# Two token streams in one transformer kernel: the context stream's mixer and feed-forward part moved beside the latent feed-forward part, and every engine's order set by a list scheduler

## The chip, the cores and the metric

The kernel runs on one core of one Trainium2 chip. The metric is the device time of one execution in microseconds (us). Three runs of the kernel before gave 1917.36, 1915.74 and 1923.25 us, a median of 1917.36.

## The reference, cut to what matters

Two layers work on two streams of tokens: 512 latent tokens (x) and 256 context tokens (ctx), both 1024 wide, with the same weights. All of it is float32.

```python
for i in range(DEPTH):                                   # DEPTH = 2
    h_l = rmsnorm(x, norm1_g[i]) * (1.0 + sc1_l) + sh1_l
    h_c = rmsnorm(ctx, norm1_g[i]) * (1.0 + sc1_c) + sh1_c
    p_l = h_l @ w_in[i]
    p_c = h_c @ w_in[i]
    ...
    k_all = jnp.concatenate([k_c, k_l], axis=1)          # latent queries read context and latent keys
    v_all = jnp.concatenate([v_c, v_l], axis=1)
    att_l = diff_attention(q_l, k_all, v_all, lam, subln_g[i], lam_init)
    x = x + g1_l * mix_out(p_l, att_l, hy_params, sg_params, w_out[i])   # hyena | sgu | attention
    x = x + g2_l * swiglu(rmsnorm(x, norm2_g[i]) * (1.0 + sc2_l) + sh2_l, ffn_w1[i], ffn_w2[i])
    if not last:
        att_c = diff_attention(q_c, k_c, v_c, lam, subln_g[i], lam_init)
        ctx = ctx + g1_c * mix_out(p_c, att_c, hy_params, sg_params, w_out[i])
        ctx = ctx + g2_c * swiglu(rmsnorm(ctx, norm2_g[i]) * (1.0 + sc2_c) + sh2_c, ffn_w1[i], ffn_w2[i])
return x
```

A mixer has three head groups: a long convolution done by small Fourier matrices (hyena), a gated spatial mixing (sgu) and differential attention. In layer 0 both streams go through everything. In layer 1 the context stream gives only its keys and values. So nothing of the latent stream in layer 0 needs more of the context stream than its keys and values of layer 0, and the rest of the context stream's layer 0 is first needed for its keys and values of layer 1.

## The kernel before

**Arithmetic.** Activations stand transposed, 128 of the width on the partitions and the tokens along the row. Each float32 operand is split in a high and a low part (`split`, L232 on ACT and L233 on DVE, some on POOL), and a product is three matmuls (`mm3`, L251 to L253) of one 128x128 block each, 512 columns wide for the latent stream and 256 for the context stream and for token-major projections. Weights arrive by DMA from the SP queue into `FW` (L240) and are split into `RW`, which holds three pairs of 128x1024.

**Tasks.** The program is written as Python generators that give up control at small steps: `lat_task` (latent stream), `con_task` (context stream), `side_task` (the filters' spectra, L905 and L906) and `ada_task` (modulation vectors, matmuls of L400). `woven` always resumes the one that has the smallest cost counted so far, divided by a rate; the rates are the tables `CON`, `SIDE`, `ADA` by phase, and `WOVEN` inside the latent mixer. So the tables and the code's order decide in which order work is written down; the tile framework's scheduler then sets each engine's order from it and places the waits. Every engine runs its queue in order.

**Stages.** From 0 to about 612 us the mixers of both streams in layer 0 run woven together: the latent one by `lat_mixer`, the context one by `con_front` (keys, queries, values, attention), `hyena`, `sgu` and `outproj`. From about 612 to 1195 us one `ffn` serves both streams in layer 0: a weight block is loaded and split once, then used for 512 latent and 256 context columns (six rounds of hidden blocks, `ROUNDS[1]`). From 1195 to 1550 us the latent mixer of layer 1 runs, with the context's keys and values in it, and from 1550 us to the end the latent FFN of layer 1 (four rounds).

**Places that the prediction names.** `norm` sums squares with a matmul against ones (L279), takes a reciprocal root in small DVE steps (`rsqrt`, L261 to L267) and spreads it with transposes (L293). In `attend`, scores take three matmuls over 64 partitions, then DVE takes the maximum (L686), ACT the exponential (L691), DVE joins the two halves (L697), and PE transposes the result (L706). `fwd` of the hyena ends in adds on DVE (L1037) and splits (L1039, L1041) on which the next matmuls wait. `AHEAD` says for how many hidden blocks the first half of the tokens is done before the second half's norm is ready ("W": weights in `RW`, "R": weights kept in `R`): one in layer 0, four in layer 1. `POOL` says which element-wise work goes to GpSimd.

## Time and profile before

| | us |
|---|---|
| median of three runs | 1917.36 |
| the profiled execution's own time | 1918.05 |
| its span, first to last instruction | 1916.3 |
| TensorE (PE) busy in it | 1797.2 |
| VectorE (DVE) busy | 1079.3 |
| ScalarE (ACT) busy | 676.9 |
| GpSimd (POOL) busy | 118.0 |

The mean granted TensorE clock was 0.963 of full speed. HBM was read at 221.18 MB and written at 22.41 MB over the span. Matmuls are pipelined and their ends are modelled in the records: one matmul lasts longer than the step to the next one's start, so the busy time of PE says where it stood still, not how fast it could be.

### The profile page before, as it was taken

To read this page: it belongs to the slowest core of one execution; us is meant where nothing else is said; L and a number is where in the kernel's file an instruction comes from. 1 tells how busy PE (TensorE), PEld (TensorE's weight loads), DVE (VectorE), ACT (ScalarE), POOL (GpSimd) and SP (SyncE) were. 2 spreads that over 40 slices of the span, in tenths; PEclk is the share of its full clock that TensorE was granted. 3 is DMA by queue.
4 is the path that set the end of the run, shared out by engine and by line. 5 is a ranking of instruction groups with operands and counts; after the bars stand their busy time and mean duration, and the time that the engine had idled before them with its cause. 6 is when DMAs were issued, how large, how long until landed. Compare 5 with 4: busy or idle time off the path is not lost.

```text
span 1916.3 us, 27513 instructions
## 1 busy us (share of the span) xinstructions
PE 1797.2 (94%) x10938; PEld 1532.3 (80%) x10938; DVE 1079.3 (56%) x2243; ACT 676.9 (35%) x1167; POOL 118.0 (6%) x127
## 2 busy tenths in 40 slices
PE   4799898888997999999999999899999999999999
PEld 1478798677776888888888888789988798888887
DVE  5677786876868533332323244779588773333333
ACT  2534434443535321212121222633455452222221
POOL 1100223311001000000000000011000000000000
PEclk9799899799997999999999999899999899999999
DMA  8667644335454434343424135453213222323321
GB/s 274 198 222 237 212 155 133 111 101 162 144 174 137 153 99 136 90 136 110 149 86 146 61 112 174 138 171 124 72 43 111 73 62 64 115 83 102 93 93 65
DMA packets 101819, 245.39 MB, mean 128 GB/s; under 512 B 9748, under 2 KB 21750, under 8 KB 101690
## 3 DMA queue, kind: packets, MB, share of 16 engines
q1 hardware_dynamic: 93450, 221.71, 36.3%
q0 software_dynamic: 8240, 21.92, 3.9%
q8 instruction: 86, 1.41, 0.3%
q14 instruction: 43, 0.35, 0.1%
HBM read 221.18 MB, written 22.41 MB: 127 GB/s over the span
## 4 chain that ended last, share of the span: by engine, by line
PE 72%; DVE 7%; ACT 2%; issue 1%; DMA 1%; POOL 0%; DVEq 0%; ACTq 0%
PE banks L251 23%; PE banks L252 22%; PE banks L253 22%; PE banks L706 1%; PE banks L400 1%; DVE tiny L686 1%; PE banks L279 1%; DMA F<-x_ctx 1%; DVE F L459 1%; DVE RW L233 0%; ACT F L506 0%; ACT F L691 0%; DVE F L1028 0%; DVE F L1189 0%; DVE F L1026 0%
## 5 line engine op out<-in xcount | busy, mean ns | idle before, releaser
L251 PE MATMUL banks<-R,RW 128*128 128x512 f32 (+1 forms) x1984 | 698.3, 353 | 8.1 <-ACT R L507 2.9
L252 PE MATMUL banks<-R,RW 128*128 128x512 f32 (+1 forms) x1984 | 695.2, 351 | 2.6 <-DVE R L510 2.6
L253 PE MATMUL banks<-R,RW 128*128 128x512 f32 (+1 forms) x1984 | 693.4, 350 | 1.7 <-DVE RW L233 1.7
L232 ACT ACTIVATE RW<-FW 128x1024 fp32r<-128x1024 f32 (+2 forms) x240 | 240.3, 1002 | 563.9 <-PE banks L252 427.5
L251 PEld LDWEIGHTS banks<-R,RW 128*128 128x128 f32 x1984 | 379.0, 191 | 66.8 <-issue 5.6
L252 PEld LDWEIGHTS banks<-R,RW 128*128 128x128 f32 x1984 | 378.8, 191 | 51.9 <-DVE R L510 3.9
L253 PEld LDWEIGHTS banks<-R,RW 128*128 128x128 f32 x1984 | 378.1, 191 | 50.1 <-DVE RW L233 2.1
L233 DVE TENSOR_TENSOR RW<-FW,RW 128x1024 fp32r<-128x1024 f32 (+2 forms) x228 | 263.1, 1154 | 243.5 <-ACT RW L232 225.7
L1189 DVE SCALAR_TENSOR_TENSOR F<-banks,mods,F 128x512 f32<-128x512 f32 (+1 forms) x192 | 116.3, 615 | 177.1 <-PE banks L253 150.6
L251 PE MATMUL banks<-R 128*128 128x256 f32 (+3 forms) x584 | 185.0, 336 | 30.7 <-ACT R L1039 12.3
L252 PE MATMUL banks<-RW,R 128*128 128x256 f32 x624 | 178.9, 287 | 2.3 <-DVE RW L233 2.2
L251 PE MATMUL banks<-RW,R 128*128 128x256 f32 x624 | 180.1, 289 | 0.8 <-ACT RW L232 0.7
L253 PE MATMUL banks<-RW,R 128*128 128x256 f32 x624 | 179.0, 287 | 0.0
L252 PE MATMUL banks<-R 128*128 128x256 f32 (+3 forms) x584 | 176.6, 316 | 0.0
L253 PE MATMUL banks<-R 128*128 128x256 f32 (+3 forms) x584 | 175.2, 312 | 1.3 <-DVE R L1041 1.3
L251 PEld LDWEIGHTS banks<-R 128*128 128x128 f32 (+1 forms) x584 | 114.8, 205 | 55.9 <-ACT R L1039 14.6
L1207 DVE TENSOR_TENSOR F<-F,banks 128x256 f32<-128x256 f32 (+1 forms) x71 | 40.0, 565 | 203.8 <-PE banks L253 189.9
L232 ACT ACTIVATE R<-F 128x512 fp32r<-128x512 f32 (+1 forms) x133 | 71.8, 550 | 222.9 <-DVE F L1207 159.8
L252 PEld LDWEIGHTS banks<-R 128*128 128x128 f32 (+1 forms) x584 | 117.5, 205 | 8.8 <-issue 3.0
L252 PEld LDWEIGHTS banks<-RW,R 128*128 128x128 f32 x624 | 120.8, 194 | 4.6 <-DVE RW L233 3.7
L251 PEld LDWEIGHTS banks<-RW,R 128*128 128x128 f32 x624 | 120.8, 194 | 3.7 <-issue 1.0
L253 PEld LDWEIGHTS banks<-RW,R 128*128 128x128 f32 x624 | 120.9, 194 | 0.7 <-issue 0.2
(158 smaller groups left out, 1681.1 us busy)
## 6 DMA issues: line engine op xcount, KB each, us to landing
FW<-in_ffn_w SPq DMA_DIRECT2D x104, 512.0 KB, 3.7
FW<-in_ada_w SPq DMA_DIRECT2D x96, 512.0 KB, 5.3
FW<-in_w_in_tm SPq DMA_DIRECT2D x50, 512.0 KB, 4.7
R<-in_tab POOLq DMA_DIRECT2D x28, 512.0 KB, 5.9
FW<-in_w_in_cm SPq DMA_DIRECT2D x24, 512.0 KB, 4.7
F<-x_ctx SPq DMA_DIRECT2D x36, 256.0 KB, 3.4
FW<-in_ffn_w SPq DMA_DIRECT2D x24, 384.0 KB, 3.1
x_ctx<-F SPq DMA_DIRECT2D x32, 256.0 KB, 2.4
```

Source lines behind the costliest of these rows:

```text
L232: self.nc.scalar.activation(hi, src, AF.Copy)
L233: (lo_eng or self.nc.vector).tensor_tensor(lo, src, hi.bitcast(F32), op=ALU.subtract)
L251: mm(out, lhsT=lh, rhs=rh, start=(i == 0), stop=False)
L252: mm(out, lhsT=lh, rhs=rl, start=False, stop=False)
L253: mm(out, lhsT=ll, rhs=rh, start=False, stop=(i == n - 1))
L279: nc.tensor.matmul(p1[:, t:t + 1], lhsT=sq[:, t * P:(t + 1) * P], rhs=self.ones[:, 0:1], start=True, stop=True)
L400: nc.tensor.matmul(pa[32 * j:32 * j + 32, :], lhsT=self.cv[:, k, :], rhs=ws[j // 2][:, j % 2, z], start=(k == 0), stop=(k == KT - 1), tile ...
L459: nc.vector.tensor_tensor(st.acc[:, cols], st.acc[:, cols], q.ap, op=ALU.add)
L686: nc.vector.tensor_reduce(m, b.ap, axis=AX.X, op=ALU.max)
L706: nc.tensor.transpose(p[:, i, z, :], ws[z][:, (a + i) * P:(a + i + 1) * P], self.ident)
L1189: self.nc.vector.scalar_tensor_tensor(x, p, self.mods[l][:, sec * 8 + k, st.v:st.v + 1], x, op0=ALU.mult, op1=ALU.add)
L1207: nc.vector.tensor_tensor(s.ap, s.ap, u, op=ALU.mult)
```

## The change

**What is computed when.** `con_front` gives only keys and values in layer 0, as in layer 1, and writes them to DRAM. The context stream then waits for "lat mixed", which the latent stream sets after the first halves of its FFN blocks. Only then it loads ctx again, norms it a second time, loads its keys and values, and does queries (`queries`, new), attention, sgu, hyena, output projection, second norm and its own FFN, and then the norm, keys and values of layer 1. All this is written between the latent stream's FFN of layer 0 and the start of its mixer of layer 1. The two streams' FFNs of layer 0 are two calls now, in four rounds each: every weight block of that layer is loaded and split twice. The latent FFN of layer 0 has four hidden blocks ahead, as layer 1 had. The spectra for 256 and for layer 1 also wait for "lat mixed". All work of POOL but one of the hyena's products (8 multiplies) goes to DVE.

**Who sets the order.** The program's calls are no longer issued as they come: `Plan` notes them all, works out from the memory they touch which needs which, gives each a duration, and plays the five engines forward; on each engine it always takes, of the calls that are ready, the one with the lowest rank (three quarters its place in the code, one quarter the length of what hangs on it). Then it issues them in that order and ties each call to the one before on its engine, so that the framework keeps the order. All instructions now have the line of `issue` (L1611).

```diff
-ROUNDS = [[(0, 6), (6, 6), (12, 5), (17, 5)], [(0, 4), (4, 4), (8, 4), (12, 4), (16, 3), (19, 3)]]
+ROUNDS = [[(0, 6), (6, 6), (12, 5), (17, 5)]]
...
-CON = [9.69, 5.75, 2, 0.75, 1.53, 5, 22.61]
+CON = [4, 5.75, 2, 6, 40, 20, 22.61]
...
+BESIDE = 14.0
+PAUSE = 12.0
...
-        "parity": (1, 0),
-        "product 1": (1, 1),
-        "product 2": (1, 0),
-        "mix": (0, 2)}
+POOL = {"in cm": (0, 0), "in tm": (0, 0), "out": (0, 0), "rope": (0, 0), "parity": (0, 0),
+        "product 1": (1, 0), "product 2": (0, 0), "mix": (0, 0)}
...
-AHEAD = ["W", "RRRW"]
+AHEAD = ["RRRW", "RRRW"]
...
+    def queries(self, st, l, j, rope):
+
+        n = st.T // 64
+        yield from self.claim(n)
+        st.held[j] += n
+        yield from self.room(*[2] * st.nt, 2)
+        gq = self.qk(st, l, 5 + j, 0, rope)
+        st.q[j] = next(gq)
...
+class Plan:
...
+    PE, DVE, ACT, POOL, SP = range(5)
+    RATE, LINE, HANDOVER, DRAIN, LANDING, WINDOW = 2.4, 258.0, 38.0, 163.0, 1620.0, 3413.0
+    COLD, WARM, ROWS = 0.5, 0.9, 100.0
...
+        rank = [self.share * k / n - (1 - self.share) * rest[k] / top for k in range(n)]
...
+    def issue(self):
+
+        nosync = mybir.DependencyInfo(mybir.DependencyClass.NoSync, mybir.DependencyReason.DATA)
+        last = [None] * 5
+        for k in self.order():
+            e, calls = self.todo[k][:2]
+            for op, args, kw in calls:
+                ins = getattr(getattr(self.tc.nc, Program.engines[e]), op)(*args, **kw).ins
+                if last[e] is not None:
+                    self.tc.add_manual_dep(ins, last[e], nosync, reason="order")
+                last[e] = ins.name
...
-        yield from con_front(0, False)
-        yield from net.hyena(con, 0, kd[0, CTX], ready=lambda: wait((0, CTX)))
-        yield from net.sgu(con, 0)
+        yield from con_front(0)
+        yield from wait("lat mixed")
+        yield from net.room(2, 2, 2, 2)
+        net.load_x(con)
+        yield from start(con, 0, 0, True)
+        for j in range(2):
+            yield from net.kv_load(con, j, kvd[0])
+            yield from net.queries(con, 0, j, False)
+            yield from net.attend(con, 0, j, [con])
...
+        yield from net.sgu(con, 0)
+        yield from net.hyena(con, 0, kd[0, CTX], ready=lambda: wait((0, CTX)))
         net.drop_h(con)
...
-        yield from mark("con")
-        yield from wait("ffn")
+        net.rates["con"] = BESIDE
+        yield from net.pause(PAUSE)
+        yield from net.ffn([con], 0, ROUNDS[0], (), True)
...
-        ff = net.ffn([lat, con], 0, ROUNDS[1], AHEAD[0], True, lambda: wait("con"))
+        ff = net.ffn([lat], 0, ROUNDS[0], AHEAD[0], True)
         yield from lat_mixer(0, ff, WOVEN[0])
         phase(3)
+        yield from take(ff, len(AHEAD[0]))
+        done.add("lat mixed")
```

**Three places in the order of PE.** In the names, `R` and `RW` hold split activations and weights, `F` unsplit ones, `ones` and `inv` belong to a norm, `ident` is the identity for transposes, and `banks` is where sums are gathered. The number at the end of a row is how many equal instructions follow each other.

The first norm of layer 1, where the latent FFN of layer 0 ends. Before:

```order
L252 MATMUL banks<-R,RW 128x256
L253 MATMUL banks<-R,RW 128x256
L279 MATMUL banks<-ones_102,F 128x1 x6
L293 MATMUL banks<-ident_100,inv 128x128 x4
L251 MATMUL banks<-R,RW 128x512 x3
L252 MATMUL banks<-R,RW 128x512
```

After:

```order
L1611 MATMUL banks<-R,RW 128x512
L1611 MATMUL banks<-R,RW 128x256 x62
L1611 MATMUL banks<-ones_86,F 128x1
L1611 MATMUL banks<-R,RW 128x256
L1611 MATMUL banks<-ones_86,F 128x1 x3
L1611 MATMUL banks<-R,RW 128x256 x17
L1611 MATMUL banks<-ident_85,inv 128x128 x4
L1611 MATMUL banks<-R,RW 128x256 x13
L1611 MATMUL banks<-R,RW 128x512 x14
L1611 MATMUL banks<-R,RW 128x256 x15
```

Between the ones-matmuls and the `inv` transposes of the latent norm stood nothing; now the context FFN's matmuls (256 columns) stand there, 17 in a row, 62 ahead of it and 13 behind it.

The end of the latent mixer of layer 0: the last steps of the latent attention, from the last scores to the first matmuls of what follows. Before:

```order
L252 MATMUL banks<-R 128x256
L253 MATMUL banks<-R 128x256
L706 MATMUL banks<-ident_100,F 128x128 x8
L905 MATMUL banks<-R 128x512
L706 MATMUL banks<-ident_100,F 128x128 x4
L906 MATMUL banks<-R 128x512
L905 MATMUL banks<-R 128x512
L251 MATMUL banks<-R 128x256
```

After:

```order
L1611 MATMUL banks<-R 128x256 x14
L1611 MATMUL banks<-ident_85,F 128x128
L1611 MATMUL banks<-R 128x256
L1611 MATMUL banks<-ident_85,F 128x128 x6
L1611 MATMUL banks<-R 128x256 x12
L1611 MATMUL banks<-ident_85,F 128x128 x4
L1611 MATMUL banks<-R 128x256 x18
L1611 MATMUL banks<-ones_86,F 128x1 x2
L1611 MATMUL banks<-R 128x256 x3
L1611 MATMUL banks<-ones_86,F 128x1 x2
L1611 MATMUL banks<-R 128x256 x34
L1611 MATMUL banks<-ident_85,inv 128x128 x4
```

Before, the `ident` transposes of the last attention (L706) had only single matmuls of the spectra (L905, L906) beside them. Now latent FFN matmuls of 256 columns, with weights kept in `R`, stand around them: the rows of 14, 1, 12, 3, 34 are the FFN's, the row of 18 is the attention's own product.

The latent FFN of layer 0. Before, with both streams on the same weights:

```order
L251 MATMUL banks<-R,RW 128x512
L252 MATMUL banks<-R,RW 128x512
L253 MATMUL banks<-R,RW 128x512
L251 MATMUL banks<-R,RW 128x256
L252 MATMUL banks<-R,RW 128x256
L253 MATMUL banks<-R,RW 128x256
```

After, in the part where the context's attention runs:

```order
L1611 MATMUL banks<-R,RW 128x512 x3
L1611 MATMUL banks<-R 128x256 x5
L1611 MATMUL banks<-R,RW 128x512 x12
L1611 MATMUL banks<-ident_85,F 128x128
L1611 MATMUL banks<-R,RW 128x512 x5
L1611 MATMUL banks<-ident_85,F 128x128 x3
L1611 MATMUL banks<-R,RW 128x512 x4
L1611 MATMUL banks<-R 128x256
L1611 MATMUL banks<-R,RW 128x512 x6
L1611 MATMUL banks<-R 128x256 x5
L1611 MATMUL banks<-ones_86,F 128x1 x2
L1611 MATMUL banks<-R,RW 128x512 x2
```

Before, PE had 512 and 256 columns of the same weights in turn; now the latent FFN's matmuls of 512 columns surround the scores, transposes (`ident`) and products of the context's attention.

## Rows read from the trace of the kernel before

**Rows 1.** Page, part 1: busy us (share of the span) xinstructions
```profile
PE 1797.2 (94%) x10938; PEld 1532.3 (80%) x10938; DVE 1079.3 (56%) x2243; ACT 676.9 (35%) x1167; POOL 118.0 (6%) x127
```

**Rows 2.** Windows by stretch: us, each engine's busy us (xinstructions), PEclk, DMA share, GB/s
```profile
0.00:96.00 96.00, 57.78 (x280) 30.74 (x281) 60.03 (x134) 40.62 (x73) 12.24 (x21) 0.86 0.71 236
96.00:612.00 516.00, 462.46 (x3200) 392.22 (x3199) 381.86 (x923) 225.53 (x428) 78.85 (x76) 0.93 0.52 165
612.00:1195.00 583.00, 581.71 (x3556) 506.01 (x3555) 215.07 (x338) 134.30 (x209) 8.54 (x11) 1.00 0.38 120
1195.00:1550.00 355.00, 333.51 (x2137) 296.58 (x2136) 279.14 (x640) 174.68 (x309) 18.33 (x19) 0.94 0.33 103
1550.00:1908.00 358.00, 357.97 (x1757) 303.88 (x1756) 141.74 (x210) 101.80 (x148) 0.00 (x0) 1.00 0.28 86
1908.00:1916.30 8.30, 3.80 (x17) 2.81 (x15) 1.50 (x2) 0.00 (x0) 0.00 (x0) 1.00 0.15 63
```

**Rows 3.** Timeline, PE, FFN of layer 1: start us, us, engine, line, form
```profile
1639.64 0.39 PE L251 MATMUL banks<-R,RW 128*128 128x512 f32 x1
...
1644.85 0.39 PE L253 MATMUL banks<-R,RW 128*128 128x512 f32 x1
```

**Rows 4.** Timeline, PE, FFN of layer 0
```profile
699.76 0.28 PE L251 MATMUL banks<-R,RW 128*128 128x256 f32 x1
...
703.96 0.28 PE L253 MATMUL banks<-R,RW 128*128 128x256 f32 x1
704.17 1.07 PE L400 MATMUL banks<-FW,cv 128*32 128x256 f32 x16
```

**Rows 5.** Groups by line and form, PE: xcount | busy us, mean ns | idle before
```profile
L251 PE MATMUL banks<-R,RW 128*128 128x512 f32 x1200 | 473.5, 395 | 3.8 <-ACT R L507 2.9 <-ACT F L555 0.9
L251 PE MATMUL banks<-R,RW 128*128 128x256 f32 x784 | 224.7, 288 | 4.2 <-DVE F L1189 2.4 <-DVE R L233 1.0 <-ACT R L232 0.8
L251 PE MATMUL banks<-RW,R 128*128 128x256 f32 x624 | 180.1, 289 | 0.8 <-ACT RW L232 0.7
L251 PE MATMUL banks<-R 128*128 128x256 f32 x432 | 129.6, 310 | 19.8 <-ACT R L1039 8.6 <-ACT R L507 3.9 <-ACT F L691 3.8
L400 PE MATMUL banks<-FW,cv 128*32 128x256 f32 x768 | 71.5, 421 | 23.7 <-DMA FW<-in_ada_w 23.7
```

**Rows 6.** Waits of PE, 96 to 612: us in total, times, longest
```profile
PE banks L251 <- ACT R L1039: 7.4, 4, 3.7
PE banks L706 <- DVE F L697: 5.9, 4, 4.0
PE banks L706 <- DVE F L482: 4.0, 1, 4.0
```

**Rows 7.** Windows around two norms and the last attention
```profile
576.00:612.00 36.00, 25.13 (x120) 19.93 (x121) 27.47 (x73) 18.12 (x39) 5.05 (x7) 0.72 0.50 154
1200.00:1224.00 24.00, 16.14 (x71) 13.31 (x70) 18.68 (x52) 13.18 (x21) 0.53 (x1) 0.72 0.51 142
1512.00:1548.00 36.00, 29.05 (x154) 25.70 (x151) 27.75 (x69) 22.19 (x47) 0.00 (x0) 0.72 0.13 41
```

**Rows 8.** Waits of PE, 0 to 96
```profile
PE banks L400 <- DMA FW<-in_ada_w: 17.7, 6, 9.5
PE banks L859 <- DMA F<-in_feats: 8.0, 1, 8.0
```

**Rows 9.** Groups by line and form, DVE and ACT: splits and multiplies
```profile
L233 DVE TENSOR_TENSOR RW<-FW,RW 128x1024 fp32r<-128x1024 f32 x172 | 211.8, 1232 | 200.5 <-ACT RW L232 182.9 <-PE banks L400 11.5 <-DMA FW<-in_ada_w 4.2
L232 ACT ACTIVATE RW<-FW 128x1024 fp32r<-128x1024 f32 x184 | 194.6, 1059 | 451.2 <-PE banks L252 334.1 <-PE banks L253 43.3 <-issue 42.7
L233 DVE TENSOR_TENSOR RW<-FW,RW 128x768 fp32r<-128x768 f32 x40 | 38.2, 954 | 26.1 <-ACT RW L232 26.0
L232 ACT ACTIVATE RW<-FW 128x768 fp32r<-128x768 f32 x40 | 33.8, 845 | 75.1 <-PE banks L252 62.5 <-issue 7.8 <-DMA FW<-in_w_out 3.9
```

**Rows 10.** DMA issues of the whole run: xcount, KB each, us to landing
```profile
FW<-in_ffn_w SPq DMA_DIRECT2D x104, 512.0 KB, 3.7
```

More of the change, by code (lines that the diff above doesn't have):

```diff
@@ L1 @@
+import heapq
 import math
@@ L127 @@
 UNITS = {"R": 104, "RW": 24, "F": 44, "FW": 24}
-CON = [9.69, 5.75, 2, 0.75, 1.53, 5, 22.61]
-SIDE = [2.59, 3, 8.68, 2.5, 5.1, 16.97, 0.64]
-ADA = [3.0, 0.6, 1.74, 0.52, 8.5, 2, 2]
+CON = [4, 5.75, 2, 6, 40, 20, 22.61]
+SIDE = [2.59, 3, 2, 4, 5.1, 16.97, 0.64]
+ADA = [3.0, 0.6, 1.74, 0.9, 8.5, 2, 2]
+BESIDE = 14.0
+PAUSE = 12.0
 WOVEN = [[11.5, 12.75, 10.55, 5.68, 7.8, 6.8, 3.47, 5.43, 8.37, 16.82],
          [8.7, 11.57, 10, 5.22, 3.19, 2.44, 5.22, 7.5, 49.17, 6.8]]
-POOL = {"in cm": (0, 1),
-        "in tm": (0, 0),
-        "out": (0, 1),
-        "rope": (0, 0),
-        "parity": (1, 0),
-        "product 1": (1, 1),
-        "product 2": (1, 0),
-        "mix": (0, 2)}
+POOL = {"in cm": (0, 0), "in tm": (0, 0), "out": (0, 0), "rope": (0, 0), "parity": (0, 0),
+        "product 1": (1, 0), "product 2": (0, 0), "mix": (0, 0)}
 START = [("F", 1), ("B", 1), ("K", 1), ("D", 1), ("F", 1), ("L", 1), ("F", 1), ("X", 1), ("A", 2), ("L", 1), ("A", 4)]
 FIRST = 2
-AHEAD = ["W", "RRRW"]
+AHEAD = ["RRRW", "RRRW"]
 class Net:
@@ L193, in room, with pause @@
         while not self.F.fits(sizes):
+            yield "wait"
+    def pause(self, work):
+        until, tries = self.cost + work, 0
+        while self.cost < until and tries < 200:
+            tries += 1
             yield "wait"
@@ L635, in kqv @@
                 pass
+        yield
+    def queries(self, st, l, j, rope):
[5 more added lines that the diff above has]
+        st.q[j] = next(gq)
+        yield
+        for _ in gq:
+            pass
         yield
@@ L1221, in ffn @@
         need = lead.T // 256
+        most = max(nf for _, nf in rounds)
+        yield from self.claim(per * most)
         for r, (f0, nf) in enumerate(rounds):
-            yield from self.claim(per * nf)
             acts, held = [], []
@@ L1277, in ffn @@
                 free(b)
-            self.unclaim(per * nf)
+        self.unclaim(per * most)
 class Pair:
@@ L1347, in network @@
 def network(ctx, tc, A):
+    tc = Plan(tc)
     net = Net(ctx, tc, A)
@@ L1383, in spectra, with con_front @@
         done.add((l, L))
-    def con_front(l, last):
+    def con_front(l):
         for j in range(2):
-            yield from net.kqv(con, l, j, False, not last)
+            yield from net.kqv(con, l, j, False, False)
             net.kv_io(con, j, kvd[l], True)
             done.add((l, "kv", j))
-            if last:
-                for b in con.k[j] + con.vv[j]:
-                    b.free()
-                net.unclaim(con.held[j])
-            else:
-                yield from net.attend(con, l, j, [con])
+            for b in con.k[j] + con.vv[j]:
+                b.free()
+            net.unclaim(con.held[j])
+        net.drop_h(con)
     def con_task():
@@ L1402, in con_task @@
         yield from mark((0, "tables"))
-        yield from con_front(0, False)
+        yield from con_front(0)
[7 more added lines that the diff above has]
+            yield from net.attend(con, 0, j, [con])
+        net.rope_tables(1)
+        done.add((1, "tables"))
+        yield from net.sgu(con, 0)
         yield from net.hyena(con, 0, kd[0, CTX], ready=lambda: wait((0, CTX)))
-        yield from net.sgu(con, 0)
         net.drop_h(con)
-        yield from wait((0, "mod1"))
         yield from net.outproj(con, 0, list(range(4)))
@@ L1415, in con_task @@
         yield from start(con, 1, 0, False)
-        yield from con_front(1, True)
-        net.drop_h(con)
+        net.drop_x(con)
+        yield from net.pause(PAUSE)
+        yield from con_front(1)
     def lat_mixer(l, ff, w):
@@ L1455, in lat_task @@
         net.drop_x(lat)
-        ff = net.ffn([lat, con], 0, ROUNDS[1], AHEAD[0], True, lambda: wait("con"))
+        ff = net.ffn([lat], 0, ROUNDS[0], AHEAD[0], True)
         yield from lat_mixer(0, ff, WOVEN[0])
         phase(3)
+        yield from take(ff, len(AHEAD[0]))
+        done.add("lat mixed")
         yield from wait((0, "mod2"))
         yield from ff
-        done.add("ffn")
         phase(4)
         net.drop_h(lat)
-        net.rope_tables(1)
-        done.add((1, "tables"))
         yield from wait((1, "mod0"))
@@ L1477, in side_task @@
         yield from spectra(0, SEQ)
+        yield from wait("lat mixed")
         yield from spectra(0, CTX)
-        yield from wait("late")
         yield from spectra(1, SEQ)
@@ L1513, in network @@
               (ada, "ada")))
+    tc.issue()
 def flat(ap):
```

209 lines of the change are left out of this document (added).

## The prediction, made before the changed kernel ran

> **What bounds the kernel now.** I read the busy times first: PE is busy for 94% of the span, DVE for 56%, ACT for 35% [rows 1]. A busy PE may still be slow, so I next asked how fast it can go. In the FFN of layer 1, 23 steps from one 512-column matmul to the next take 1644.85 - 1639.64 = 5.21 us, 0.2265 us each [rows 3]. In the FFN of layer 0, 35 steps of 256 columns take 703.96 - 699.76 = 4.20 us, 0.120 us each [rows 4]. In both places the granted clock is 1.00, the level of 2.4 GHz, and PE never stands [rows 2]. So I count what PE needs at that pace. By form there are 3 x 1200 matmuls of 512 columns and 3 x (784 + 624 + 432) = 5520 of 256 (the lines L252 and L253 have the same counts as L251) [rows 5]; the same view has 232 and 240 more over 64 rows or from the spectra. That is 3832 x 0.2265 = 868 and 5760 x 0.120 = 691. The 768 matmuls of L400 take between 1.07/16 = 0.067 [rows 4] and 71.5/768 = 0.093 each [rows 5]; I take 0.07, nearer to the steady place, so 54. Some 570 transposes and ones, which step by 0.11 us, give 63, the first filters 8. The need is about 1684 us of 1916: some 230 us are lost.
>
> Where they are lost the windows by stretch show [rows 2]. Counted in the same way, the needs of the six stretches are about 40, 405, 577, 302, 358 and 4 us. The losses are then 56 in the start (0 to 96), about 110 in the two mixers of layer 0 (96 to 612), 6 in the FFN of layer 0, 53 in the mixer of layer 1, none in its FFN, and 4 at the end. Part of it is idle PE (38, 54, 1, 21, 0 and 4 us: width less busy), part is the slow clock: a mean of 0.93 over 516 us means up to 36 us given away at the 1.2 GHz level; the rest is short handovers. Waits of PE in the mixers are short and many: the largest are 7.4 us in four for the hyena's splits and 5.9 us in four for the joined attention weights [rows 6]. Three places lose most for their length: 576 to 612 (PE busy 25.13 of 36 at a clock of 0.72), 1200 to 1224 (16.14 of 24) and 1512 to 1548 (29.05 of 36) [rows 7]: the two ends of a mixer, and the norm that opens layer 1. The start waits for DMAs of modulation weights, 17.7 us, and of the first filter inputs, 8.0 us [rows 8].
>
> One rule would size this otherwise. Rows 2 show PE's weight loads busy for 303.88 of 358 us, 85%, in a stretch where nothing can be gained. The Trainium skill (Perfetto Trace Analysis, "Identifying the Most-Contended Engine") would judge PE's headroom by that share and not by matmul time; by it the headroom would be 1916 - 1532 = 384 us, and half of it back would give 1725. The trace does not bear it out: 85% is full here, so the sum goes by the pace.
>
> **The change part by part.** PE's need stays: 144 matmuls of 512 columns become 288 of 256 (four blocks ahead instead of one), 288 x 0.120 - 144 x 0.2265 = 2 us. What changes is where it stands. I cut the new order of PE at the latent stream's second norm in layer 0, at the context FFN's last matmul, and at the second norm in layer 1, and count by the same steps: A, start and latent mixer, 367 us; B, latent FFN with the whole rest of the context stream, 669; C, latent mixer of layer 1, 299; D, last FFN, 345. Before, the need up to the same first cut (612 us) was 40 + 405 = 445: the context's mixer (about 90) has gone to B, and 17 of FFN blocks ahead have come.
>
> A. The start still waits for the same 8 MB of modulation weights. The new order of ACT scales the latent stream's normed rows (8 times two steps of 128x512) ahead of the context's, which stood first before, so the latent hyena's projections can start earlier; I take 10 of the 56 us back (0 to 20). The end, 576 to 612, lost 20 us; the second order excerpt puts FFN matmuls (14, 12, 3 and 34 of 0.120 us) into the attention's steps, where the two waits of L706 were 4.0 us each [rows 6]. I leave 8. The other 90 of the 110 shrink with the need that is left (327 of 405) to 73, if the order were no better. The new order mixes key and query projections with the hyena's and the scores' matmuls one by one, which is what the waits of rows 6 lack; I leave 40 (between 20 and 73). A = 367 + 46 + 8 + 40 = 461.
>
> B. The stretch it grows from ran without loss [rows 2]. The context's chains (norms, softmax, transposes) now stand among independent 512-column matmuls, as the third excerpt shows, and for the attention steps there are 5 to 22 of them, 1 to 5 us, between steps. I allow 10 us (0 to 40): 679. The cover for what is added here is PE's own work. Second splits: in the two listings DVE has 40 more of 128x1024 (12 of them were POOL's), 24 of 128x768 and 32 of 128x640: 40 x 1.232 + 24 x 0.954 + 32 x about 0.82 = 98 us; ACT has 28, 24 and 32 more: 28 x 1.059 + 24 x 0.845 + 32 x about 0.74 = 74 us [rows 9]. With the second norm of the context (about 10) and POOL's former work (about 19), DVE comes to 1079 + 127 = 1206, ACT to about 755, of some 1815: neither is the bound. In B itself DVE has 215 [rows 2] plus most of the 98 and some 115 of the context's mixer, about 420 of 679. If that cover were gone, the 98 us of DVE would come out in full. The queues: SP gets 44 more loads of 512 KB and about 12 MB of second-matrix blocks, loses 68 transfers of the context's x (17 MB), so about 20 MB more in all, 265 MB in 1.8 ms or 147 GB/s, where the first 96 us moved 236 GB/s [rows 2]; a load lands 3.7 us after its issue [rows 10]. POOL issues six more small loads and does less else. Cost beside PE: nothing.
>
> C. Of 53 us lost, about 20 stood at the norm that opens the layer (1200 to 1224 and what follows) and 18 at the end [rows 7]. The first order excerpt puts 17 context FFN matmuls (2.0 us) between the norm's two steps and some 75 around them; I leave 2 there. The end has the same four blocks ahead as before, now woven in: 10. The other 15 I cut to 12. C = 299 + 24 = 323. D = 345 + 5 = 350.
>
> The sum is 461 + 679 + 323 + 350 = 1813 us of span; the profiled execution was 1.75 us longer than its span, which gives 1815. That execution, 1918.05, stands 0.7 us above the median of the runs, so nothing is corrected.
>
> **The rivals.**
>
> First, the order is no better than before: each mixer keeps its loss. A = 367 + 56 + 327 x 110/405 = 512, C = 299 + 52 = 351, so 512 + 679 + 351 + 350 + 2 = 1894. For it speaks that the mixers' chains are as long as before, and that the context's work, which filled gaps in layer 0, is gone; against it, that the latent mixer of layer 1, which has little beside it, loses 53 in 355, less than the 110 in 516 of the two woven mixers. This is also the case in which the change does not do what it says of the order.
>
> Second, slower: B takes on the character of the mixers. PE's queue is in order, so where a context matmul is not ready as early as the planned durations say, the latent FFN's matmuls behind it stand too, and the clock falls as in rows 7. At the mixers' rate, 110 lost on 405 of need, B would lose 182 instead of 10: 1987. It is level with before from 10 + 102 = 112 us of loss in B, one sixth of its need. For it: the planner takes a call as soon as it counts it ready, so there is hardly a margin at any of some hundred handovers. Against it: a stall pushes PE alone; DVE and ACT, with 40% to spare, run on, and the next handover then has margin. The Trainium skill (TensorE: Matmul & The Clock Gate, "What happens when you issue a matmul") says that matmuls stay in program order and only weight loads are pulled ahead; the four-us waits of L706 in rows 6 agree.
>
> Third, better: the order removes nearly all waits behind the start. A = 367 + 36 + 20 = 423, B = 674, C = 309, D = 348: 1756 with the 2 us.
>
> **How the numbers follow.** Forecast (1770 to 1860) 0.58; first rival (1860 to 1910) 0.17; second 0.12; third 0.13. The predicted time is the forecast's, 1815. The range 1750 to 1890 holds the forecast, nearly all of the third and most of the first, about 0.8. A measurement of this kernel can tell about 0.5% from no change, 1908 to 1927 here: faster 0.85 (forecast, third, most of the first), same 0.05 (the rest of the first and a mild second), slower 0.10.
>
> **What would show it.** Windows of the new profile cut at the same four points: A near 460, B near 680 with PE busy over 98% and a clock of 1.00, C near 325, D near 350. The first 96 us should lose some 10 us less. Around the first norm of layer 1 PE should not stand over 1 us. DVE should be busy about 1200 us, POOL under 40. I am wrong if PE stands in B, if DVE is above 85% busy in A or C, or if the mixers' clock falls below 0.93.

## The result and the profile after

The changed kernel took 1861.10 us (median of 1871.12, 1857.86, 1864.34 and 1857.82), the kernel before, on the same chip, 1918.67. The ratio is 0.9707 with a 95% interval of 0.9661 to 0.9752: 58 us faster. Forecast were 1815 us and a range of 1750 to 1890. The profiled execution is the one of 1871.12 us, 10 us above the median: its mean granted clock was 0.968, against 0.970 to 0.977 in the other three. So the others need not have lost all that its trace loses to the clock: at 0.977 and 0.975 the two executions at 1858 us were some 26 to 33 us less at the 1.2 GHz level (an estimate, twice the difference of the means times 1860 us), and they were 13 us faster.

Part 1 of the page after (busy us, share of the span, instructions) and the first stretch and the four cuts of the forecast as windows (us, each engine's busy us, PEclk, DMA share, GB/s; the last cut in two). PEclk is the granted clock: 1.00 is the 2.4 GHz level, 0.50 the 1.2 GHz level.

```profile
PE 1797.8 (96%) x11088; PEld 1535.3 (82%) x11088; DVE 1153.0 (62%) x2389; ACT 764.4 (41%) x1286; POOL 49.4 (3%) x81
```

```profile
0.00:96.00 96.00, 66.57 (x399) 42.15 (x399) 64.70 (x153) 44.08 (x77) 6.24 (x15) 0.86 0.79 269
96.00:459.60 363.60, 354.04 (x2490) 297.61 (x2487) 272.46 (x633) 162.09 (x297) 14.38 (x20) 0.97 0.51 167
459.60:1163.80 704.20, 691.90 (x4413) 604.62 (x4412) 416.56 (x802) 300.20 (x485) 15.92 (x30) 0.99 0.52 160
1163.80:1521.00 357.20, 341.41 (x2169) 301.71 (x2168) 273.21 (x642) 164.43 (x299) 12.81 (x16) 0.92 0.32 100
1521.00:1862.00 341.00, 341.00 (x1617) 287.15 (x1617) 124.55 (x161) 93.61 (x131) 0.00 (x0) 1.00 0.27 85
1862.00:1869.30 7.30, 2.88 (x13) 2.06 (x11) 1.50 (x2) 0.00 (x0) 0.00 (x0) 1.00 0.23 91
```

PE was busy for 1797 us before [rows 1] and is for 1798 now: the 47 us between the two spans came out of its idle time, 119 us before and 72 now. Its need, each matmul that starts in a stretch times the pace that the prediction gives its form (0.2265 us for 512 columns, 0.120 for 256), is 54, 319, 671, 299 and 343 us for start, rest of A, B, C and D, 1687 in all (forecast 1684). Width less need is the loss:

| cut | width, forecast | width, after | loss before | loss, forecast | loss, after |
|---|---|---|---|---|---|
| A: start and latent mixer, layer 0 | 461 | 460 | 168 | 94 | 86, of it 42 in the start |
| B: latent FFN and the rest of the context | 679 | 704 | 7 | 10 | 33 |
| C: latent mixer, layer 1 | 323 | 357 | 52 | 24 | 59 |
| D: last FFN, with the end | 350 | 348 | 5 | 5 | 5 |

(The losses before are counted in the same way, with the cuts at the same events of that trace: 632, 1205 and 1569 us.) The gain is A alone, 82 us. B loses 26 more than before, and C, which was to give 29 us, 7 more. Little of what C loses is idle time: its PE is busy for 341.41 of 357.20 us, at a clock of 0.92. In 5-us windows around its first attention, from 1318 us on:

```profile
1318.00:1323.00 5.00, 4.89 (x40) 4.63 (x39) 4.25 (x10) 2.69 (x6) 0.00 (x0) 1.00 0.02 5
...
1328.00:1333.00 5.00, 5.00 (x22) 3.02 (x20) 1.17 (x2) 1.83 (x4) 0.00 (x0) 1.00 0.26 79
1333.00:1338.00 5.00, 5.00 (x21) 4.16 (x21) 4.13 (x9) 3.00 (x5) 0.00 (x0) 0.63 0.15 34
1338.00:1343.00 5.00, 5.00 (x19) 4.25 (x19) 2.33 (x9) 1.08 (x2) 0.00 (x0) 0.50 0.12 48
...
1358.00:1363.00 5.00, 5.00 (x22) 4.58 (x22) 3.70 (x8) 0.63 (x1) 0.00 (x0) 0.50 0.00 0
1363.00:1368.00 5.00, 5.00 (x37) 5.00 (x37) 0.50 (x2) 0.75 (x2) 0.00 (x0) 0.80 0.00 0
```

At 1328 PE is busy without a break, at the 2.4 GHz level, and yet starts 22 matmuls where it started 40 ten us earlier; from 1334 on the clock is at the 1.2 GHz level for 31 us, although PE is on record as busy all through. From 1332 to 1368 us C loses 17 us. What runs at 1328 to 1333 the timeline of PE shows (start us, us, engine, line, op, names, rows*columns of weights, output):

```profile
1329.81 0.39 PE L1611 MATMUL banks<-RW,R 128*128 128x256 f32 x1
1330.13 0.50 PE L1611 MATMUL banks<-R 64*128 64x256 f32 x2
1330.56 0.39 PE L1611 MATMUL banks<-RW,R 128*128 128x256 f32 x1
1330.88 0.50 PE L1611 MATMUL banks<-R 64*128 64x512 f32 x1
1331.31 0.39 PE L1611 MATMUL banks<-RW,R 128*128 128x256 f32 x1
```

Scores over 64 rows and projections over 128 rows, one by one. From a 128-row matmul of 256 columns to the next start it is 0.32 us (1330.56 to 1330.88), not 0.120; from a 64-row one of 512 columns 0.43 (1330.88 to 1331.31), not 0.227: 0.2 us more at each change of the row count. The trace has 267 such changes, that of before 207; stretches of one matmul between two changes number 107, against 38. The planner prices a change at 100 ns (`ROWS`). The Trainium skill (TensorEngine Tiling (Array Packing), "Key Properties") says that a change of the tiling mode drains TensorE, without a price; the trace shows a price at each change of the row count, 0.2 us, and not whether it is a drain.

From this came three theories (explanations to be told apart by experiments) for the 46 us above the forecast. **Theory 1**: changes of rows and the clock that falls behind dense ones. **Theory 2**: the attention's chain on DVE and ACT, for which the mixers have no other work left. **Theory 3**: the pinned order leaves no margin at the handovers.

### The profile page after: what moved, and what is told of

It reads as the page before. It is cut to its first block, busy times and chain, and to the rows that moved or that the text cites. A ratio compares the mean times of both kernels' runs of the same rounds, so it can differ in the third digit from the quotient of the medians.

```text
span 1869.3 us, 28221 instructions
## 1 busy us (share of the span) xinstructions
PE 1797.8 (96%) x11088; PEld 1535.3 (82%) x11088; DVE 1153.0 (62%) x2389; ACT 764.4 (41%) x1286; POOL 49.4 (3%) x81
## 2 busy tenths in 40 slices
DMA packets 101920, 264.31 MB, mean 141 GB/s; under 512 B 10101, under 2 KB 20055, under 8 KB 101787
## 4 chain that ended last, share of the span: by engine, by line
PE 62%; issue 7%; DVE 4%; ACT 3%; DMA 1%; POOL 0%; SPq 0%; ACTq 0%; DVEq 0%; POOLq 0%
PE banks L1611 62%; DVE F L1611 2%; ACT F L1611 1%; DVE RW L1611 1%; ACT R L1611 1%; ACT RW L1611 1%; DVE tiny L1611 1%; DVE R L1611 0%; DMA R<-in_tab 0%; DMA kd<-F 0%; DMA F<-in_sg_norm_g 0%; POOL R L1611 0%; SPq L1611 0%; ACTq L1611 0%; DVEq L1611 0%
## 5 line engine op out<-in xcount | busy, mean ns | idle before, releaser
L1611 PE MATMUL banks<-R,RW 128*128 128x512 f32 (+1 forms) x5808 | 1139.7, 349 | 8.6 <-ACT R L1611 2.4
L1611 PEld LDWEIGHTS banks<-R,RW 128*128 128x128 f32 x5808 | 937.4, 189 | 156.4 <-issue 7.9
L1611 DVE TENSOR_TENSOR RW<-FW,RW 128x1024 fp32r<-128x1024 f32 (+2 forms) x318 | 351.0, 1107 | 329.1 <-ACT RW L1611 298.7
L1611 ACT ACTIVATE RW<-FW 128x1024 fp32r<-128x1024 f32 (+2 forms) x318 | 306.9, 967 | 581.8 <-PE banks L1611 493.0
L1611 PE MATMUL banks<-R 128*128 128x256 f32 (+4 forms) x2080 | 381.9, 322 | 19.3 <-ACT R L1611 7.0
L1611 PEld LDWEIGHTS banks<-R 128*128 128x128 f32 (+1 forms) x2080 | 305.3, 202 | 74.7 <-issue 20.6
L1611 PE MATMUL banks<-RW,R 128*128 128x256 f32 x1872 | 272.3, 292 | 2.3 <-ACT F L1611 1.0
L1611 PEld LDWEIGHTS banks<-RW,R 128*128 128x128 f32 x1872 | 247.5, 195 | 16.0 <-issue 7.1
L1611 ACT ACTIVATE R<-F 128x256 fp32r<-128x256 f32 (+2 forms) x246 | 123.0, 519 | 148.0 <-DVE F L1611 130.4
L1611 DVE TENSOR_TENSOR R<-F,R 128x256 fp32r<-128x256 f32 (+3 forms) x246 | 131.9, 553 | 45.9 <-ACT R L1611 45.3
L1611 DVE SCALAR_TENSOR_TENSOR F<-banks,mods,F 128x512 f32<-128x512 f32 (+1 forms) x160 | 97.3, 614 | 100.6 <-PE banks L1611 99.3
L1611 ACT ACTIVATE F<-banks 128x256 f32<-128x256 f32 (+1 forms) x199 | 94.2, 485 | 140.4 <-PE banks L1611 109.3
L1611 DVE TENSOR_TENSOR F<-F,banks 128x256 f32<-128x256 f32 (+1 forms) x180 | 85.1, 499 | 85.0 <-PE banks L1611 64.5
L1611 DVE TENSOR_TENSOR F<-F 128x256 f32<-128x256 f32 (+2 forms) x227 | 117.0, 546 | 9.3 <-ACT F L1611 3.7
L1611 ACT ACTIVATE F<-banks,tiny,rq 128x768 f32<-128x768 f32 (+1 forms) x80 | 72.3, 906 | 68.7 <-DVE tiny L1611 67.0
L1611 ACT ACTIVATE R<-banks 128x512 fp32r<-128x512 f32 (+1 forms) x114 | 53.7, 510 | 78.7 <-PE banks L1611 77.3
L1611 PE MATMUL banks<-ident,F 128*128 128x128 f32 x360 | 71.8, 305 | 9.6 <-ACT F L1611 4.3
L1611 DVE TENSOR_REDUCE tiny<-banks 128x1 f32<-128x768 f32 (+1 forms) x80 | 66.9, 843 | 22.8 <-PE banks L1611 22.5
L1611 DVE TENSOR_TENSOR R<-banks,R 128x512 fp32r<-128x512 f32 (+1 forms) x114 | 62.7, 576 | 18.4 <-ACT R L1611 18.0
L1611 PE MATMUL banks<-FW,cv 128*32 128x256 f32 x768 | 59.5, 430 | 9.5 <-DMA FW<-in_ada_w 7.5
L1611 PEld LDWEIGHTS banks<-ident,F 128*128 128x128 f32 x360 | 47.3, 154 | 24.0 <-ACT F L1611 6.6
L1611 ACT ACTIVATE F<-F 128x256 f32<-128x256 f32 (+1 forms) x92 | 41.2, 459 | 43.7 <-DVE F L1611 25.6
```

The lines of the kernel that those rows point to most:

```text
L1611: ins = getattr(getattr(self.tc.nc, Program.engines[e]), op)(*args, **kw).ins
```

## The experiments

All ratios are to the kernel before in the same runs. Losses by cut (us) are from each kernel's profiled execution, counted as above; the kernels with the old flow have their cuts at the same events. That execution is 10 us above the median for the changed kernel, and at most 3 us off it for the others of the table. A change of rows is a step from a 128-row to a 64-row matmul or back.

| kernel | median us | ratio (95%) | A | B | C | D | changes of rows |
|---|---|---|---|---|---|---|---|
| kernel before | 1918.7 | 1 | 168 | 7 | 52 | 5 | 207 |
| changed kernel | 1861.1 | 0.9707 (0.9661 to 0.9752) | 86 | 33 | 59 | 5 | 267 |
| e1, no list | 1878.8 | 0.9777 (0.9739 to 0.9816) | 105 | 41 | 37 | 6 | 203 |
| e2, old flow with list | 1933.5 | 1.0084 (1.0057 to 1.0111) | 167 | 8 | 64 | 5 | 251 |
| e3, rows kept 3 us | 1841.4 | 0.9586 (0.9551 to 0.9621) | 79 | 29 | 40 | 5 | 107 |
| e12, rows kept 1 us | 1844.1 | 0.9619 (0.9589 to 0.9650) | 80 | 29 | 39 | 5 | 177 |
| e5, margin | 1855.6 | 0.9677 (0.9653 to 0.9702) | 84 | 36 | 40 | 6 | 265 |
| e6, one block ahead | 1907.5 | 0.9947 (0.9922 to 0.9971) | 95 | 55 | 62 | 5 | 255 |
| e7, halves together | 1843.7 | 0.9617 (0.9593 to 0.9640) | 95 | 36 | 55 | 5 | 131 |
| e8, halves and rows | 1858.5 | 0.9711 (0.9675 to 0.9747) | 104 | 36 | 63 | 5 | 95 |
| e9, rows and margin | 1847.1 | 0.9638 (0.9608 to 0.9669) | 82 | 34 | 39 | 5 | 103 |
| e10, halves and margin | 1856.7 | 0.9689 (0.9658 to 0.9720) | 102 | 38 | 60 | 6 | 137 |
| e11, context later | 1851.8 | 0.9661 (0.9626 to 0.9697) | 83 | 28 | 48 | 5 | 103 |

**Which half of the change earns what.** The new flow without the list:

```diff
-    tc = Plan(tc)
...
-    tc.issue()
```

> The change without its list scheduler: the new place of the context's work, the new weights and the new table of engines stay, but the calls go out in the order in which the program makes them. Theory A (the list order is what fills the latent mixers; the move of the context takes filler away from them): the mixers lose at least what they lost before, 110 and 53 us, and more, for the context is gone from them; the stretch with the latent feed-forward part loses 35 us or somewhat more; together 1890 to 1930 us. Theory B (moving the context does most of it, the list little): within 15 us of the changed kernel, 1850 to 1875 us.

It took 1878.8 us, between the two. Moving the context and what goes with it (the blocks ahead, the second splits, POOL's work on DVE) gives some 40 us by itself, the list 13 (by the ratios, whose intervals just overlap) to 18 (by the medians) more. Of what goes with the move only the blocks ahead were undone by themselves (e6, below). In the profiled executions the list takes 19 us of loss out of A and 8 out of B, and puts 22 into C (37 to 59), part of it the half clock above: in layer 1's mixer the order as the program writes it loses least of all kernels here.

The list without the new flow, the kernel before with `Plan` put over it:

```diff
+    tc = Plan(tc)
...
+    tc.issue()
```

> The kernel before, its work in its old places, with the list scheduler alone put over it. Theory A (the list order earns most in the mixers wherever the context stands): 1860 to 1890 us, the mixers' loss falls from 163 us to about 110 to 130. Theory B (moving the context does most of it): 1895 to 1920 us, near the kernel before.

Both theories were wrong: 0.8% slower than before. A loses as much as before (167, 168 before), the FFN next to nothing, and C 64 instead of 52: it is again layer 1's mixer in which the list loses. So the list is worth minus 15 us on the old flow and plus 13 to 18 on the new one. It is not a better order as such.

**The changes of rows.** The price of one by itself: the changed kernel with 432 matmuls of 256 columns behind its last one.

```diff
+        blocks = [(full,), (lo,), (full, lo), (full,), (full, full, lo, lo), (full,), (lo, hi), (full,), (full, lo)]
+        for i, block in enumerate(blocks):
+            for j in range(48):
+                r = block[j % len(block)]
+                ins = nc.tensor.matmul(out[(full, lo, hi).index(r)][:, :256], lhsT=op[r, :P], rhs=op[r], start=True, stop=True).ins
```

> The changed kernel with 432 matmuls of 256 columns added behind its last one, in nine blocks of 48, which nothing reads: 128 rows; the lower 64 rows; 128 and 64 rows in turn; 128; two of 128 and two of 64 in turn; 128; lower and upper 64 rows in turn; 128; 128 and 64 in turn. Theory 1: blocks of one row count step by 0.12 us at full clock, blocks in turn by 0.3 us or more, blocks in pairs by about 0.2 us. If the step is about 0.12 us in all blocks, a change of rows costs nothing by itself, and the long steps in the trace have another cause. Lower and upper rows in turn: 0.12 us if they run one after the other, down to 0.06 us if they run beside each other.

It ran once. The windows of its trace over five of the blocks (128 rows, the lower 64, in turn in two windows, in pairs, lower and upper half in turn):

```profile
1866.60:1872.40 5.80, 5.80 (x49) 5.70 (x47) 0.75 (x1) 0.00 (x0) 0.00 (x0) 1.00 0.22 90
1872.40:1878.30 5.90, 5.90 (x49) 5.80 (x48) 0.00 (x0) 0.00 (x0) 0.00 (x0) 1.00 0.01 3
1878.30:1881.30 3.00, 3.00 (x12) 1.78 (x10) 0.00 (x0) 0.00 (x0) 0.00 (x0) 1.00 0.00 0
1881.30:1900.30 19.00, 19.00 (x39) 10.63 (x39) 0.00 (x0) 0.00 (x0) 0.00 (x0) 0.53 0.00 0
...
1908.70:1918.90 10.20, 10.20 (x50) 7.07 (x49) 0.00 (x0) 0.00 (x0) 0.00 (x0) 1.00 0.01 2
...
1924.90:1927.90 3.00, 3.00 (x49) 2.93 (x48) 0.00 (x0) 0.00 (x0) 0.00 (x0) 1.00 0.02 5
```

Alone, each kind steps by 0.120 us. In turn the start-to-start step is 0.31 us at the 2.4 GHz level: 0.19 us for a change. In pairs the mean is 10.2/48 = 0.213 us, and with a change at every second matmul that is again 0.19 each. After 3.9 us in turn the clock falls to the 1.2 GHz level, and the step becomes 0.51 us, with PE busy 19.00 of 19.00 us; in pairs it stays at 1.00 over the 10 us. The second block in turn did the same after 2.9 us. So in the probe both halves of theory 1 stand: a change costs 0.19 us, and a dense run of them brings the clock down, which no idle time in the records shows. Lower and upper half in turn take 3.0/48 = 0.06 us each: they run beside each other. Ahead of the blocks this kernel runs the changed kernel's order, and its trace has the stretch at half clock again, 31 us from 1336 on; its C loses 58.

Then the same cause taken out of the kernel. PE goes on with ready calls of the row count that it has just run, for up to 3 us, before it changes:

```diff
+    def alike(can, todo, rows):
+        best = min((x for x in can if todo[x[1]][10] == rows), default=can[0])
...
-            k = self.pick(can[e], todo, turn[self.POOL] > now + 150) if e == self.DVE else heapq.heappop(can[e])[1]
+            k = self.pick(can[e], todo, turn[self.POOL] > now + 150) if e == self.DVE else heapq.heappop(can[e])[1] if e or now - since > self.KEEP else self.alike(can[e], todo, rows)
```

> The changed kernel with one rule more in its scheduler: TensorE goes on with calls of the row count that it has just run for up to 3 us, as long as one is ready, before it takes one of another row count. This lowers its changes between 64-row scores and 128-row matmuls from 267 to 107. Theory 1 (the loss in the layer 1 mixer is these changes, about 0.2 us each, and the clock that falls after a stretch of them): 160 changes fewer by 0.2 us is 32 us off, and up to 30 us at half clock in the layer 1 mixer is in doubt besides; 1815 to 1840 us, the layer 1 mixer 325 to 340 us instead of 357. Theory 2 (the mixer waits for the chain of scores, softmax and its sums on VectorE and ScalarE, and there is no filler, since the context has ended): longer runs of one kind delay that chain further; 1855 to 1875 us, the layer 1 mixer 355 us or more. Theory 3 (the order pinned without margin is at fault): no change beyond 0.5%, 1853 to 1870 us.

1841.4 us, 20 below the changed kernel, and 107 changes. C is 338 us wide and loses 40. Its first attention, as far into the stretch as the windows at 1328 to 1363 above:

```profile
1318.00:1330.00 12.00, 12.00 (x93) 10.80 (x91) 11.75 (x39) 4.99 (x11) 0.00 (x0) 1.00 0.01 2
1330.00:1342.00 12.00, 11.18 (x90) 10.64 (x90) 11.67 (x34) 8.26 (x15) 0.00 (x0) 1.00 0.12 34
1342.00:1354.00 12.00, 11.64 (x86) 10.24 (x85) 9.25 (x19) 5.74 (x13) 0.00 (x0) 1.00 0.12 33
```

PE now has idle moments that it did not have (11.18 of 12.00), and starts 90 matmuls in 12 us where it started 45 or so: the chain of the attention shows, where the changes and the half clock had covered it. With the limit at 1 us instead of 3:

> Rows kept for up to 1 us instead of 3: 177 changes of rows, between the 267 of the changed kernel (1861 us) and the 107 of the kernel with rows kept for 3 us (1841 us). Theory 1 in its plain form (each change costs 0.2 us, and the clock follows): 90 changes fewer, 56% of the way, 1846 to 1854 us. Theory 1 with the clock as the larger part (half clock follows only the densest runs, and 1 us breaks those already): 1838 to 1846 us. If the number of changes is not what counts: 1853 to 1870 us.

1844.1 us with 177 changes. The first 90 changes fewer gave 17 us, the next 70 gave 3 or nothing (the intervals overlap). At 0.19 us each they would have given 17 and 13. What e12 and e3 have in common is that changes after a single matmul are gone (11 and 3 of them, against 107), and with them the dense runs: at most 6 and 4 changes in any 5 us, 14 in the changed kernel. Above 1 us, what is saved on changes comes back as waiting: C has 98 changes in the changed kernel, 74 here and 38 in e3, and here and in e3 it loses the same.

**Margin.** The planner's allowance for a handover between engines:

```diff
-    RATE, LINE, HANDOVER, DRAIN, LANDING, WINDOW = 2.4, 258.0, 38.0, 163.0, 1620.0, 3413.0
+    RATE, LINE, HANDOVER, DRAIN, LANDING, WINDOW = 2.4, 258.0, 150.0, 163.0, 1620.0, 3413.0
```

> The changed kernel with the scheduler's allowance for a handover between two engines at 150 ns instead of 38. Theory 3 (the pinned order is too tight; a call that comes later than planned holds up its whole engine, and that is the loss of 35 us in the stretch with the latent feed-forward part): that stretch goes from 704 to 685 us, the whole to 1835 to 1850 us. Theory 1 (changes of rows and the clock): 265 changes instead of 267, so nothing gained; 1855 to 1875 us, or some us more where the fillers now run out earlier.

1855.6 us, 5 less and within the two intervals; B, where theory 3 put the gain, loses 36 instead of 33. C loses 40, as little as with rows kept, but with 94 changes in it (265 in all); the run of single changes at 1320 to 1332 is nearly as dense (12 in 5 us, against 13 in the changed kernel's at 1329), but the clock fell for 3 us and not for 31 behind it. In windows there:

```profile
1320.00:1332.00 12.00, 12.00 (x66) 8.52 (x65) 7.87 (x14) 5.96 (x12) 0.00 (x0) 1.00 0.11 33
1332.00:1344.00 12.00, 12.00 (x66) 10.35 (x66) 9.85 (x29) 6.25 (x11) 0.00 (x0) 0.86 0.10 34
1344.00:1356.00 12.00, 12.00 (x92) 11.12 (x91) 11.96 (x36) 5.48 (x11) 0.00 (x0) 1.00 0.00 0
```

So most of what C gained here and with rows kept, 19 us, is the stretch at half clock (17 us lost from 1332 to 1368) and not the price of the changes one by one; the order of e5, hardly less dense, was spared most of it. Both traces of the changed kernel's order have it. The two executions at 1858 us had, by their clocks, about that much less time at the 1.2 GHz level; whether it was this stretch no trace shows. Against them, rows kept are still 16 us faster. Rows kept and margin together:

> Rows kept for up to 3 us and the handover allowance of 150 ns together: 103 changes of rows. The kernel with rows kept took 20 us off by itself and the allowance alone 5. Theory 1 (both took the same thing away, the half clock behind dense changes of rows; the allowance only happened to shorten the one dense run of the layer 1 mixer): no more than the rows alone, 1836 to 1846 us. Theory 3 (the margin is worth something by itself): 1830 to 1837 us.

1847.1 us, slower than the rows alone (their intervals just overlap). No run shows a worth of the margin by itself; theory 3 falls.

**Blocks ahead.** The changed kernel with one FFN block ahead in layer 0:

```diff
-AHEAD = ["RRRW", "RRRW"]
+AHEAD = ["W", "RRRW"]
```

> The changed kernel with one piece of the feed-forward part ahead of the layer 0 mixer's end instead of four, as before the change. If the prediction's term for the layer 0 mixer's tail is right (8 us of loss left there, 20 before), the stretch to the second norm of layer 0 loses 10 to 15 us more, 1870 to 1880 us in all. If the other moved work fills that tail as well: no change, 1855 to 1865 us.

1907.5 us: 46 lost, most of what the change gains, where 10 to 15 were expected. A loses 9 more, B 22 more. Around the cut between them, at 455 us, and last the same stretch of the changed kernel:

```profile
432.00:456.00 24.00, 14.61 (x97) 13.35 (x95) 16.23 (x52) 9.96 (x20) 2.12 (x4) 0.80 0.35 101
456.00:480.00 24.00, 22.69 (x102) 19.78 (x103) 10.80 (x23) 12.59 (x25) 0.00 (x0) 0.77 0.15 45
480.00:528.00 48.00, 39.73 (x179) 31.05 (x178) 31.52 (x74) 20.67 (x40) 1.60 (x3) 0.89 0.40 123
...
432.00:528.00 96.00, 94.99 (x696) 84.73 (x694) 62.26 (x158) 47.27 (x95) 4.23 (x8) 0.99 0.50 151
```

432 to 528 lose 35 us here, against 4 in the changed kernel. The edit does two things: it takes FFN blocks from the mixer's tail, and it lets the context begin three blocks earlier, for "lat mixed" is set behind them. Which of the two costs more was not taken apart.

**The scores' halves together.** Since the halves run beside each other, the six matmuls of a source can go out as one piece, lower and upper in turn (the planner counts the piece as one call, at half the pace):

```diff
+                    bs, off = [self.ps("S", nk) for _ in range(2)], 0
+                    for s in reversed(srcs):
+                        for x, y in ((0, 0), (0, 1), (1, 0)):
+                            for c in range(2):
...
-                        b = self.ps("S", nk)
...
-                            self.mm3(b[:, off:off + s.T], [(q[r, qt * P:(qt + 1) * P], s.k[j][h][r, :])])
...
+                        b = bs[c]
```

> The changed kernel with the scores of the two 64-row halves of a head issued in turn, lower and upper rows, the six of one source as one piece of the order; in the probe such matmuls ran beside each other, 0.061 us each. TensorE needs about 36 us less (432 score matmuls, 288 of 512 and 144 or more of 256 columns at half their step), and changes of rows fall from 267 to 131. Theory 1 (rows and the clock they cost): at least the 20 us of the kernel with rows kept, up to 45; 1815 to 1842 us. Theory 2 (the attention's chain on VectorE and ScalarE and the four banks of the scores bound the mixers): TensorE's saved time turns into idle time, and both halves hold their banks at once; 1845 to 1870 us.

(The counts in that text should read 192 of 512 columns and 240 of 256, which is the 36 us.) 1843.7 us: 17 off, no more than the changes of rows alone are worth. Need fell by 38 us to 1648, but the loss rose, from 182 to 191 us in all: 95 in A (86 in the changed kernel), and C, with 40 changes instead of 98 and without the long stretch at half clock, still lost 55. PE's idle time in C went from 16 to 26 us. The largest waits of PE in C (us in total, times, longest), of the changed kernel and of this one:

```profile
PE banks L1611 <- ACT F L1611: 8.0, 4, 3.5
PE banks L1611 <- ACT R L1611: 5.7, 3, 3.9
PE banks L1611 <- DVE F L1611: 1.5, 4, 0.7
...
PE banks L1621 <- DVE F L1621: 8.8, 4, 4.2
PE banks L1621 <- ACT F L1621: 8.8, 6, 3.5
PE banks L1621 <- ACT R L1621: 5.8, 3, 3.9
```

Theory 2 fits what is left once the row changes are fewer: PE's saved time turned into waits for DVE and ACT, which do the softmax and its sums. With rows kept, or with margin, it got worse:

> The halves together, and rows kept for up to 3 us as well: 95 changes of rows. Theory 1: as the halves together, and 36 changes fewer are 7 us more off at most; 1805 to 1840 us. Theory 2: the longer runs hold up the chain, no gain over the halves alone; 1845 to 1870 us.

> The halves together with the handover allowance of 150 ns. Theory 2, for this kernel (the mixers are held by the chain from scores over softmax to the next scores, and an order that expects longer handovers puts other work between them): 1828 to 1840 us, against 1843.7 with the halves alone. If the four banks of the scores are what binds, the order can't help: 1840 to 1850 us.

1858.5 and 1856.7 us. They lose 102 to 104 in A and 60 to 63 in C. The two halves of a head hold all four score banks (2 to 5) at once; that this is what stops the next scores was not shown by itself.

**More other work for C.** Rows kept, and the context's FFN slower beside the latent one:

```diff
-BESIDE = 14.0
+BESIDE = 9.0
```

> Rows kept, and the weight with which the context's feed-forward part is woven beside the latent one at 9 instead of 14, so that more of it is left when the latent part is done and layer 1 opens. Theory 2 (the losses at the opening norm, 8 us, and at the first steps of the layer 1 mixer, 8 us, come from a lack of other work there): 8 to 12 us off the 1841 us of the kernel with rows kept, 1828 to 1836 us. If what waits there is the program's order (the context's keys and values are due before the latent attention and have no slack to give): the loss moves with the work, 1838 to 1855 us.

1851.8 us, 10 slower than the rows alone. The norm that opens layer 1 loses some 4 us where it lost 8, but C loses 48 instead of 40; at 1210 us, in it, PE stands for 5.0 us and waits for ACT. The loss moved with the work, as the second reading expected; that it is the context's keys and values that are due there was not shown by itself.

The best of these is e3, rows kept for 3 us: 1841.4 us, 0.9586 of the kernel before, 20 us better than the changed kernel.

## Why the prediction was right, and where not

The sign and the range held; the time was 46 us too low.

- **What bounds it.** Need by pace came out at 1687 of a forecast 1684. The last FFN stands at the pace without loss (341 of 341 us busy), with weight loads busy 287.15 of 341.00, 84%. So what the prediction took from the Trainium skill (Perfetto Trace Analysis, "Identifying the Most-Contended Engine"), PE's headroom by the share of its weight loads, is answered as before: 84% is full here.
- **A** was right, 460 for 461, the last few us by luck: need is 6 above the forecast and loss 8 below it. The start loses 42 of 57 before (10 were to come back, 15 came; the wait for modulation weights fell from 17.7 us [rows 8] to 7.5). The rest loses 45 where 48 were forecast. The tail's gain of 12 us for the blocks ahead was about right where it was put: undone (e6), A loses 9 more. But the whole loses 46 by the medians, and of what the profiled executions show of it most, 22 us, stands behind the tail, in B. What the prediction allowed in B, 10 us of loss, silently rested on these blocks, or on the later start that comes with them.
- **B** was mis-sized: the step "I allow 10 us" measured 33, still inside the bounds that the prediction gave (0 to 40). The covers that were named held: DVE 417 us in B (420 forecast), DMA 264.31 MB in all (265). But the context's chains do not vanish among independent matmuls. At 696 to 731 us, where its hyena runs, 10 us went, and 8 at the norm that opens layer 1:

```profile
696.00:708.00 12.00, 10.59 (x68) 8.29 (x68) 8.67 (x21) 3.23 (x7) 1.06 (x2) 1.00 0.72 229
708.00:719.00 11.00, 6.76 (x40) 4.87 (x39) 9.19 (x23) 3.16 (x6) 0.53 (x1) 0.89 0.52 158
719.00:731.00 12.00, 12.00 (x62) 11.34 (x61) 6.46 (x16) 3.55 (x7) 1.59 (x3) 0.68 1.01 315
```

PE waited 1.4 us for a table of the Fourier matrices, 1.9 for DVE and 2.3 for ACT, then ran at a clock of 0.68. That reads like the second rival's mechanism (a late call holds the FFN matmuls behind it), at a small part of its price (182 us in B). The stretch of half clock behind it, 10 us, is in the traces with margin (e5) and with rows kept (e3) too, so what would remove it stays open.
- **C** failed: 59 us of loss instead of 24. The step was "the other 15 I cut to 12", and in A the sentence that the order "mixes key and query projections with the hyena's and the scores' matmuls one by one", taken there as a gain. Mixing them one by one is what cost: 19 of the 59 go when rows are kept (e3, and e12), and most of them are the half clock that a dense run of changes brought (e4, e5). The price of a change was in the trace of before (207 changes) and was not looked for. Of the 40 that remain, 17 stand at the end, 1464 to 1500, where 10 were forecast:

```profile
1464.00:1500.00 36.00, 28.11 (x147) 24.28 (x147) 29.19 (x71) 22.81 (x47) 0.00 (x0) 0.72 0.14 41
```

It reads like 1512 to 1548 before (29.05 busy, 0.72) [rows 7]: the same blocks ahead, and nothing gained by weaving them: that stretch lost 17 as well. Around the opening norm, where PE should not stand over 1 us, it stood 2.4.
- **D** was right: 348 for 350.
- **The list's worth.** The prediction credited the order with what lies between the first rival (the order is no better, 1894 us) and the forecast, 79 us. By e1 the list is worth 13 to 18. Without it A loses 105, not the 145 of that rival, so most of what the prediction gave the order came with the move of the work, some 40 of the 58 us; and C, with the list, loses more than the rival's 52.
- **What would show it.** A and D came as said, the start somewhat better. DVE came to 1153, not 1200, POOL to 49, not under 40; PE was busy 1798 of the 1869 us, so neither bounds the span. Of the three signs of being wrong, the mixers' clock under 0.93 came true (0.92 in C), and PE standing in B in part: 12 us in all, still 98% busy. DVE was 73% and 76% busy in A and C.

## What to carry to other kernels

A list scheduler that takes whatever is ready next may alternate between matmuls of different row counts, as this one did (267 changes, 207 before). Measure what a change costs, and give the scheduler a rule that keeps it on one row count for a microsecond, before trusting its order; whether the true price in its plan, 0.19 us instead of 0.10, would have done as much was not tried. Count need by pace and loss by stretch: a PE that is busy all through can still run at half its speed, and here the starts per microsecond and the granted clock said so. Work moved under a stretch without loss brings its own chains along, and the blocks that bridge the seam between the stretches can be worth as much as the move (46 us here, with the later start that comes with them).

## What the runs showed of the hardware

- A change between 128-row and 64-row matmuls of 256 columns cost TensorE 0.19 us, in the probe singly and in pairs alike (steps of 0.31 and 0.213 us against 0.120).
- Matmuls of alternating row count brought the granted clock from the 2.4 to the 1.2 GHz level, after 3.9 and 2.9 us in the two blocks of the probe (19 us at 0.53), although no idle time is recorded; with a change at every second matmul it stayed at 1.00 for the 10 us. It came back in the block of one row count that followed.
- Matmuls over the lower and the upper 64 rows in turn, into different banks, ran beside each other: 0.061 us each at 256 columns, in the probe. The Trainium skill (TensorE: Matmul & The Clock Gate, "Part 3: Packing small matmuls — row/col tiling") says so of tiles at distinct rows; the probe agrees.
